# Attention in units of two heads inside a one-core hybrid layer (SSD, forgetting attention, PEER) on Trainium2

## The chip, the cores and the metric

The kernel runs on one core of one Trainium2 chip. The metric is the device time of one execution in microseconds (us). The engines are TensorE (PE; its weight loads are listed apart as PEld), VectorE (DVE), ScalarE (ACT), GpSimd (POOL) and SyncE (SP, used here to issue DMAs). Matmuls write to PSUM, which ACT and DVE read.

## The reference

For 512 tokens of width 2048 the layer computes, in float32:

```
h   = RMSNorm(x);  p = h @ w_in          (z | x,B,C | dt | q | k | v | forget logits)
y_A = Mamba-2 SSD of 16 heads
y_B = attention of 16 heads of 64:  for each block i of 128 queries
        s = q_i k[:qe]^T / 8 + C[t] - C[s],  C = cumsum(log sigmoid(f))
        p = softmax(s where t >= s);   out_i = p v[:qe]
x1  = x + concat(y_A, y_B) @ w_out
out = RMSNorm(x1 + PEER(RMSNorm(x1)))    (PEER: top-16 of 128*128 experts, 8 heads)
```

The change concerns y_B alone: 16 heads times 4 query blocks, block t (0 to 3) against its first 128(t+1) keys.

## The kernel before, in words

The large projections are computed to float32 accuracy with three matmuls: a weight piece is loaded by SP (`wload`, L73), split on ACT into a high part (L81) and on DVE into a low part (L82), and multiplied as high*high, low*high, high*low. `project_t` (L98) gives 128 output columns transposed, 16 steps of 3 matmuls of 128x512 (L103 to L105); `project_n` (L110) gives a 512-wide block of columns for all four token tiles (L117 to L119).

The attention (`fox`, L441) is a Python generator that is stepped from inside the projections, so that its PE work stands between projection matmuls. `front` (L229) computes the transposed q and k of two heads (a head pair, `hp`, 0 to 7) with `fox_qk` (L433). While it computes those of head pair hp+1, it calls `slot` after every fourth step (12 matmuls), 8 times in all, and each call advances `fox` by one step for head pair hp. The last head pair is stepped from `mid_first` (L499), the first block of the output projection, at each of its 16 steps (12 matmuls each), which also transposes the SSD output (`to_T`, L138) at its first four steps and splits the last attention rows (`split(15,7)`) when the attention is done.

One step of `fox` before starts one *unit*, (head, query block t), and advances those in flight:

- at its own slot: the score matmul (L453; 64 rows of the array, since the head has 64 elements, by 128(t+1) columns, float32, which the trace lists as two records) and the causal mask added by a bf16 matmul (L454) into the PSUM tile `at` (two buffers); then softmax: L456 and L459 on DVE, the exponential on ACT (L461), L462 and L463 on DVE;
- two slots later: t+1 transposes of the probabilities (L468, PSUM tile `tp`, two buffers) and their copy by ACT (L470);
- three slots later: t+1 value matmuls (L474, 64 columns of the array, two records each), summed in a second `tp` tile, and the copy to `mixf` by DVE (L476).

The two heads of a pair are done one after the other: four units of one, then four of the other. `crow`, the row of C of a head, is broadcast to all partitions by a DMA on SP (L487; two buffers, one per head). The order of the instructions on an engine is that of the program except where the scheduler of the language moved some, mostly around the last head pair. A matmul's form in the trace, as 64\*128, is the part of the array it uses (rows\*columns).

Of the kernel before, what the change touches and what calls it, by code (L numbers as in the profile page):

```python
# [9 lines left out]
F32 = mybir.dt.float32  # L10
# [3 lines left out]
AF = mybir.ActivationFunctionType  # L14
OP = mybir.AluOpType
AX = mybir.AxisListType
# [3 lines left out]
P = 128  # L20
T = 512
NT = 4
# [4 lines left out]
HD = 64  # L27
# [28 lines left out]
def bcast(ap, offset, dims):  # L56
    return bass.AP(tensor=ap.tensor, offset=ap.offset + offset, ap=[[0, P]] + dims)


class K:  # L60
# [380 lines left out]
    def fox(self, fp):  # L441


        nc = self.nc
        waiting = []

        def unit(hp, q, k, hh, t, crow):
            h = 2 * hp + hh
            rs = slice(hh * HD, (hh + 1) * HD)
            qe = (t + 1) * P  # L450
            ts_ = slice(t * P, qe)
            S = self.pp.tile([P, T], F32, name="at", tag="at", bufs=2)
            nc.tensor.matmul(S[:, :qe], q[rs, ts_], k[rs, :qe], start=True, stop=False, skip_group_check=True)  # L453
            nc.tensor.matmul(S[:, ts_], self.identb, self.maskb, start=False, stop=True, skip_group_check=True)  # L454
            pr = fp.tile([P, T], F32, name="pr", tag="pr", bufs=4)
            nc.vector.scalar_tensor_tensor(pr[:, :qe], S[:, :qe], self.nab[:, t, 32 + h:33 + h],  # L456
                                           crow[:, :qe], op0=OP.add, op1=OP.subtract)
            mx = fp.tile([P, 1], F32, name="mx", tag="mx", bufs=4)
            nc.vector.tensor_reduce(mx, pr[:, :qe], axis=AX.X, op=OP.max, negate=True)  # L459
            sm = fp.tile([P, 1], F32, name="sm", tag="sm", bufs=4)  # L460
            nc.scalar.activation(pr[:, :qe], pr[:, :qe], AF.Exp, bias=mx, accum_out=sm)  # L461
            nc.vector.reciprocal(sm, sm)  # L462
            nc.vector.tensor_scalar(pr[:, :qe], pr[:, :qe], sm, None, op0=OP.mult)  # L463
            yield
            yield
            tp = self.pp.tile([P, NT, P], F32, name="tp", tag="tp", bufs=2)
            for c in range(t + 1):
                nc.tensor.transpose(tp[:, c, :], pr[:, c * P:(c + 1) * P], self.ident)  # L468
            pT = fp.tile([P, NT, P], F32, name="pT", tag="pT", bufs=3)
            nc.scalar.activation(pT[:, :t + 1, :], tp[:, :t + 1, :], AF.Copy)  # L470
            yield
            yT = self.pp.tile([P, P], F32, name="tp", tag="tp", bufs=2)
            for c in range(t + 1):
                nc.tensor.matmul(yT[rs, :], self.vn[:, c, h * HD:(h + 1) * HD], pT[:, c, :],  # L474
                                 start=(c == 0), stop=(c == t), skip_group_check=True)
            nc.vector.tensor_copy(self.mixf[rs, hp, ts_], yT[rs, :])  # L476

        def advance():
            for u in waiting[:]:
                if next(u, 0) == 0:  # L480
                    waiting.remove(u)

        while True:
            hp, q, k = self.fox_in
            for hh in range(2):
                crow = fp.tile([P, T], F32, name="crow", tag="crow", bufs=2)
                nc.sync.dma_start(crow, bcast(self.rows, (32 + 2 * hp + hh) * T, [[1, T]]))  # L487
                for t in range(NT):
                    advance()
                    waiting.append(unit(hp, q, k, hh, t, crow))  # L490
                    next(waiting[-1])
                    yield
            if hp == 7:
                break
        while waiting:
            advance()
            yield

    def mid_first(self, es):  # L499


        nc, io = self.nc, self.io
        self.mixT = Th, Tl = self.new_T()

        def split(slot, c):
            nc.scalar.activation(Th[:, slot, :], self.mixf[:, c, :], AF.Copy)
            nc.vector.tensor_sub(Tl[:, slot, :], self.mixf[:, c, :], Th[:, slot, :].bitcast(F32))

        for c in range(6):
            split(c, c)  # L510

        def slot(kc):
            if kc < 4:
                for t in (2 * (kc % 2), 2 * (kc % 2) + 1):
                    self.to_T(self.mixn[:, t, (kc // 2) * 512:(kc // 2 + 1) * 512], t, Th, Tl, 7 + 4 * (kc // 2), 4)
            if kc == 4:
                split(6, 6)
            if next(self.fox_steps, 0) == 0 and not done:
                done.append(1)
                split(15, 7)  # L520

        done = []
        self.hp = self.pool(es, "h2p", side="right")
        self.xin = self.hp.tile([P, NT, 512], F32, name="xin", tag="h2n", bufs=1)
        for t in range(NT):
            nc.sync.dma_start(self.xin[:, t, :], io["x"][t][:, 0:512])
        return self.project_n(io["wo"][0], Th, Tl, slot)
# [31 lines left out]
    def mid_norm(self):  # L559

        nc, mp, x1 = self.nc, self.mp, self.x1
        self.T2 = [self.t2.tile([P, KC, DN], F32R, name=f"T2{n}", tag=f"T2{n}", bufs=1) for n in "hl"]
        self.T3 = [self.sx.tile([P, KC, P], F32R, name=f"T3{n}", tag="S", bufs=4) for n in "hl"]
        sm = mp.tile([P, NT], F32, name="sm2")
# [19 lines left out]
    def scores(self, tk):  # L584

        nc, io = self.nc, self.io
        kT = self.sx.tile([P, 16, P], F32, name="kT", tag="S", bufs=4)
        nc.sync.dma_start(kT, io["kT"])
# [3 lines left out]
        for c4 in range(4):  # L592
# [21 lines left out]
            def post(c4=c4, q=q, qn=qn):  # L614
# [3 lines left out]
                for j in range(4):  # L618
# [3 lines left out]
                    for t in range(NT):  # L622
                        nc.tensor.matmul(sp[:, t, :], q[j][:, t * P:(t + 1) * P], kT[:, hh, :], start=True, stop=True)
                    S = tk.tile([P, NT, P], F32, name="S", tag="tk_oh", bufs=3)
                    nc.scalar.activation(S, sp, AF.Copy)
# [462 lines left out]
```

## Time and profile before

| | |
|---|---|
| runs | median 3315.44 us of 3 (3312.17, 3315.44, 3324.38) |
| the profiled execution | 3313.59 us; span from first to last instruction 3311.9 us |
| PE | busy 3171.9 us, 96% |
| PEld | 2926.7 us, 88% |
| DVE | 2372.4 us, 72% |
| ACT | 1175.1 us, 35% |
| POOL | 882.6 us, 27% |
| mean granted TensorE clock | 0.988 of 2.4 GHz |

Busy time is an average over stages. The attention units lie between 436.4 us (the first score matmul) and 757.2 us (the end of the last value matmuls), a tenth of the span; what they are worth is read there. PE matmuls are pipelined and their listed durations overlap, so the cost of one is read from the distance between the starts of neighbours.

### The profile page before, as it was taken

The numbers are of one execution on the slowest core, as the hardware profiler recorded it, in microseconds if no ns is written. First come the engines' busy times: TensorE is split into PE (matmuls) and PEld (weight loads), VectorE is DVE, ScalarE is ACT, GpSimd is POOL, SyncE is SP. The second block draws the span as 40 slices with busy tenths as digits, with TensorE's granted clock in tenths as the row PEclk, the third lists the DMA queues.
The fourth block names the chain that finished last, engine by engine and source line by source line (L and its number), as shares of the span: only waits on it lengthen the run. The fifth ranks groups of instructions, "written<-read, shape, count | busy, mean of one in ns | idle before, by whom it ended". The sixth has DMA issues, their size and how long they took to land.

```text
span 3311.9 us, 45983 instructions
## 1 busy us (share of the span) xinstructions
PE 3171.9 (96%) x18153; PEld 2926.7 (88%) x18153; DVE 2372.4 (72%) x3315; ACT 1175.1 (35%) x1908; POOL 882.6 (27%) x535
## 2 busy tenths in 40 slices
PE   6999999999989988999998899999999999999998
PEld 4777776667789988999998899999999999999997
DVE  6474345553234699879877688898888998888885
ACT  3342233342232332364565432333332322323332
POOL 2000000001012054314111244434434454344430
PEclk9999999999989999999999999999999999999999
DMA  4333322215232255978877899999999999989992
GB/s 137 97 105 89 115 80 71 64 61 165 89 125 89 90 199 208 348 270 314 318 290 275 324 377 363 337 363 350 345 345 366 365 346 348 356 334 356 341 337 89
DMA packets 211400, 798.29 MB, mean 241 GB/s; under 512 B 19728, under 2 KB 27920, under 8 KB 166224
## 3 DMA queue, kind: packets, MB, share of 16 engines
q1 hardware_dynamic: 146352, 375.21, 32.9%
q0 software_dynamic: 55440, 375.15, 29.7%
q10 hardware_dynamic: 9392, 45.00, 3.3%
q8 instruction: 142, 2.33, 0.3%
q14 instruction: 74, 0.61, 0.1%
HBM read 748.98 MB, written 46.27 MB: 240 GB/s over the span
## 4 chain that ended last, share of the span: by engine, by line
PE 35%; DMA 7%; issue 5%; DVE 3%; POOL 2%; ACT 1%; DVEq 0%; POOLq 0%; ACTq 0%
PE mm L826 4%; PE mm L824 4%; PE mm L825 4%; PE mm L939 3%; PE mm L941 3%; PE mm L940 3%; DMA Gd<-gb 2%; PE at L941 2%; PE tp L941 1%; PE tp L939 1%; PE tp L940 1%; PE at L939 1%; PE at L940 1%; DMA A<-Ad 1%; DVE w_lo L82 1%
## 5 line engine op out<-in xcount | busy, mean ns | idle before, releaser
L81 ACT ACTIVATE w_hi<-w_raw 128x1024 fp32r<-128x1024 f32 x666 | 705.0, 1061 | 1552.2 <-PE mm L940 455.4
L82 DVE TENSOR_TENSOR w_lo<-w_raw,w_hi 128x1024 fp32r<-128x1024 f32 x648 | 815.6, 1270 | 533.6 <-ACT w_hi L81 523.8
L826 PE MATMUL mm<-T2h,w_lo 128*128 128x352 f32 x1664 | 543.8, 327 | 33.4 <-DVE w_lo L82 33.3
L824 PE MATMUL mm<-T2h,w_hi 128*128 128x352 f32 x1664 | 549.0, 330 | 0.8 <-ACT w_hi L81 0.8
L825 PE MATMUL mm<-T2l,w_hi 128*128 128x352 f32 x1664 | 540.7, 325 | 0.0
L753 POOL DMA_INDIRECT row<-in_u_dram,idx x128 | 207.4, 1620 | 555.8 <-DVE row L758 529.2
L826 PEld LDWEIGHTS mm<-T2h,w_lo 128*128 128x128 f32 x1664 | 316.4, 190 | 40.5 <-DVE w_lo L82 40.4
L770 DVE SCALAR_TENSOR_TENSOR x2g<-row,act,x2g 128x2048 f32<-128x2048 f32 x128 | 336.4, 2628 | 15.6 <-DMA row<-in_v_dram,idx 9.5
L939 PE MATMUL mm<-Wh,w_hi 128*128 128x352 f32 x1024 | 331.4, 324 | 0.0
L941 PE MATMUL mm<-Wh,w_lo 128*128 128x352 f32 x1024 | 331.1, 323 | 0.0
L940 PE MATMUL mm<-Wl,w_hi 128*128 128x352 f32 x1024 | 329.8, 322 | 0.0
L758 DVE SCALAR_TENSOR_TENSOR row<-row,h2n 128x2048 f32<-128x2048 f32 x128 | 305.5, 2401 | 19.0 <-DMA row<-in_u_dram,idx 19.0
L824 PEld LDWEIGHTS mm<-T2h,w_hi 128*128 128x128 f32 x1664 | 317.2, 191 | 1.1 <-ACT w_hi L81 1.1
L825 PEld LDWEIGHTS mm<-T2l,w_hi 128*128 128x128 f32 x1664 | 316.8, 190 | 0.0
L753 POOL DMA_INDIRECT row<-in_v_dram,idx x128 | 218.0, 1704 | 337.0 <-DVE x2g L770 309.9
L117 PE MATMUL mm<-w_hi,T_hi 128*128 128x512 f32 x512 | 205.0, 400 | 0.0
L119 PE MATMUL mm<-w_hi,T_lo 128*128 128x512 f32 x512 | 203.2, 397 | 0.0
L118 PE MATMUL mm<-w_lo,T_hi 128*128 128x512 f32 x512 | 201.9, 394 | 0.0
L940 PEld LDWEIGHTS mm<-Wl,w_hi 128*128 128x128 f32 x1024 | 194.0, 189 | 0.0
L941 PEld LDWEIGHTS mm<-Wh,w_lo 128*128 128x128 f32 x1024 | 193.5, 189 | 0.0
L939 PEld LDWEIGHTS mm<-Wh,w_hi 128*128 128x128 f32 x1024 | 192.9, 188 | 0.0
L103 PE MATMUL mm<-T_hi,w_hi 128*128 128x512 f32 x464 | 190.3, 411 | 0.0
(302 smaller groups left out, 6274.6 us busy)
## 6 DMA issues: line engine op xcount, KB each, us to landing
w_raw<-in_uT_dram SPq DMA_DIRECT2D x256, 512.0 KB
w_raw<-in_v_dram SPq DMA_DIRECT2D x256, 512.0 KB
w_raw<-in_wT_dram SPq DMA_DIRECT2D x58, 512.0 KB
Gd<-gb ACTq DMA_DIRECT2D x22, 1024.0 KB
G<-Gd POOLq DMA_DIRECT2D x32, 704.0 KB
w_raw<-in_wN_dram SPq DMA_DIRECT2D x32, 512.0 KB
w_raw<-in_wo_dram SPq DMA_DIRECT2D x32, 512.0 KB
w_raw<-in_wq_dram SPq DMA_DIRECT2D x32, 512.0 KB
```

The costliest lines, as they stand in the source:

```text
L81: nc.scalar.activation(hi, raw, AF.Copy)
L82: sub = eng.tensor_sub(lo, raw, hi.bitcast(F32))
L117: nc.tensor.matmul(ps[t], Th[:, kc, s], wh, start=(kc == 0), stop=False)
L753: nc.gpsimd.indirect_dma_start(out=row, out_offset=None, in_=src, in_offset=bass.IndirectOffsetOnAxis(ap=idx[:, j:j + 1], axis=0))
L758: nc.vector.scalar_tensor_tensor(row, row, 1.0, h, op0=OP.mult, op1=OP.mult, accum_out=act[:, j:j + 1])
L770: nc.vector.scalar_tensor_tensor(acc, row, act[:, j:j + 1], acc, op0=OP.mult, op1=OP.add)
L824: nc.tensor.matmul(ps, wh, Th[:, kc, :TD], start=(kc == 0), stop=False)
L825: nc.tensor.matmul(ps, wh, Tl[:, kc, :TD], start=False, stop=False)
L826: nc.tensor.matmul(ps, wl, Th[:, kc, :TD], start=False, stop=(kc == KC - 1))
L939: nc.tensor.matmul(ps[j], vh, wh, start=f, stop=False)
L940: nc.tensor.matmul(ps[j], vh, wl, start=False, stop=False)
L941: nc.tensor.matmul(ps[j], vl, wh, start=False, stop=l)
```

## The change

A unit is now (head pair, query block): both heads at once. At its slot it issues the two score matmuls one behind the other (head 0 on rows 0 to 63 of the array, head 1 on rows 64 to 127, each into an `at` tile of its own), then both masks and both softmaxes. Three slots later (before: two) come the transposes of both heads, four slots later the value matmuls, in which the heads alternate at each of the t+1 key blocks, head 0 on columns 0 to 63 and head 1 on columns 64 to 127 of one `tp` tile; one copy of 128 partitions to `mixf` replaces two of 64. A unit is started at every second slot, so that 4 units take the 8 slots that 8 units took. `crow` has three buffers in place of two, and both rows of a pair are fetched together. In `mid_first` the generator is stepped twice per step from the ninth on.

```diff
--- before.py
+++ after.py
@@ -441,39 +441,52 @@
     def fox(self, fp):
 
 
+
         nc = self.nc
         waiting = []
 
-        def unit(hp, q, k, hh, t, crow):
-            h = 2 * hp + hh
-            rs = slice(hh * HD, (hh + 1) * HD)
+        def unit(hp, q, k, t, crow):
             qe = (t + 1) * P
             ts_ = slice(t * P, qe)
-            S = self.pp.tile([P, T], F32, name="at", tag="at", bufs=2)
-            nc.tensor.matmul(S[:, :qe], q[rs, ts_], k[rs, :qe], start=True, stop=False, skip_group_check=True)
-            nc.tensor.matmul(S[:, ts_], self.identb, self.maskb, start=False, stop=True, skip_group_check=True)
-            pr = fp.tile([P, T], F32, name="pr", tag="pr", bufs=4)
-            nc.vector.scalar_tensor_tensor(pr[:, :qe], S[:, :qe], self.nab[:, t, 32 + h:33 + h],
-                                           crow[:, :qe], op0=OP.add, op1=OP.subtract)
-            mx = fp.tile([P, 1], F32, name="mx", tag="mx", bufs=4)
-            nc.vector.tensor_reduce(mx, pr[:, :qe], axis=AX.X, op=OP.max, negate=True)
-            sm = fp.tile([P, 1], F32, name="sm", tag="sm", bufs=4)
-            nc.scalar.activation(pr[:, :qe], pr[:, :qe], AF.Exp, bias=mx, accum_out=sm)
-            nc.vector.reciprocal(sm, sm)
-            nc.vector.tensor_scalar(pr[:, :qe], pr[:, :qe], sm, None, op0=OP.mult)
+            rs = [slice(hh * HD, (hh + 1) * HD) for hh in range(2)]
+            S = [self.pp.tile([P, T], F32, name="at", tag="at", bufs=2) for _ in range(2)]
+            for hh in range(2):
+                nc.tensor.matmul(S[hh][:, :qe], q[rs[hh], ts_], k[rs[hh], :qe], start=True, stop=False,
+                                 skip_group_check=True)
+            prs = []
+            for hh in range(2):
+                h = 2 * hp + hh
+                nc.tensor.matmul(S[hh][:, ts_], self.identb, self.maskb, start=False, stop=True,
+                                 skip_group_check=True)
+                pr = fp.tile([P, T], F32, name="pr", tag="pr", bufs=4)
+                nc.vector.scalar_tensor_tensor(pr[:, :qe], S[hh][:, :qe], self.nab[:, t, 32 + h:33 + h],
+                                               crow[hh][:, :qe], op0=OP.add, op1=OP.subtract)
+                mx = fp.tile([P, 1], F32, name="mx", tag="mx", bufs=4)
+                nc.vector.tensor_reduce(mx, pr[:, :qe], axis=AX.X, op=OP.max, negate=True)
+                sm = fp.tile([P, 1], F32, name="sm", tag="sm", bufs=4)
+                nc.scalar.activation(pr[:, :qe], pr[:, :qe], AF.Exp, bias=mx, accum_out=sm)
+                prs.append((pr, sm))
+            for pr, sm in prs:
+                nc.vector.reciprocal(sm, sm)
+                nc.vector.tensor_scalar(pr[:, :qe], pr[:, :qe], sm, None, op0=OP.mult)
             yield
             yield
-            tp = self.pp.tile([P, NT, P], F32, name="tp", tag="tp", bufs=2)
-            for c in range(t + 1):
-                nc.tensor.transpose(tp[:, c, :], pr[:, c * P:(c + 1) * P], self.ident)
-            pT = fp.tile([P, NT, P], F32, name="pT", tag="pT", bufs=3)
-            nc.scalar.activation(pT[:, :t + 1, :], tp[:, :t + 1, :], AF.Copy)
+            yield
+            pT = []
+            for pr, sm in prs:
+                tp = self.pp.tile([P, NT, P], F32, name="tp", tag="tp", bufs=2)
+                for c in range(t + 1):
+                    nc.tensor.transpose(tp[:, c, :], pr[:, c * P:(c + 1) * P], self.ident)
+                pT.append(fp.tile([P, NT, P], F32, name="pT", tag="pT", bufs=3))
+                nc.scalar.activation(pT[-1][:, :t + 1, :], tp[:, :t + 1, :], AF.Copy)
             yield
             yT = self.pp.tile([P, P], F32, name="tp", tag="tp", bufs=2)
             for c in range(t + 1):
-                nc.tensor.matmul(yT[rs, :], self.vn[:, c, h * HD:(h + 1) * HD], pT[:, c, :],
-                                 start=(c == 0), stop=(c == t), skip_group_check=True)
-            nc.vector.tensor_copy(self.mixf[rs, hp, ts_], yT[rs, :])
+                for hh in range(2):
+                    h = 2 * hp + hh
+                    nc.tensor.matmul(yT[rs[hh], :], self.vn[:, c, h * HD:(h + 1) * HD], pT[hh][:, c, :],
+                                     start=(c == 0), stop=(c == t), skip_group_check=True)
+            nc.vector.tensor_copy(self.mixf[:, hp, ts_], yT)
 
         def advance():
             for u in waiting[:]:
@@ -482,14 +495,17 @@
 
         while True:
             hp, q, k = self.fox_in
+            crow = []
             for hh in range(2):
-                crow = fp.tile([P, T], F32, name="crow", tag="crow", bufs=2)
-                nc.sync.dma_start(crow, bcast(self.rows, (32 + 2 * hp + hh) * T, [[1, T]]))
-                for t in range(NT):
-                    advance()
-                    waiting.append(unit(hp, q, k, hh, t, crow))
-                    next(waiting[-1])
-                    yield
+                crow.append(fp.tile([P, T], F32, name="crow", tag="crow", bufs=3))
+                nc.sync.dma_start(crow[hh], bcast(self.rows, (32 + 2 * hp + hh) * T, [[1, T]]))
+            for t in range(NT):
+                advance()
+                waiting.append(unit(hp, q, k, t, crow))
+                next(waiting[-1])
+                yield
+                advance()
+                yield
             if hp == 7:
                 break
         while waiting:
@@ -515,9 +531,10 @@
                     self.to_T(self.mixn[:, t, (kc // 2) * 512:(kc // 2 + 1) * 512], t, Th, Tl, 7 + 4 * (kc // 2), 4)
             if kc == 4:
                 split(6, 6)
-            if next(self.fox_steps, 0) == 0 and not done:
-                done.append(1)
-                split(15, 7)
+            for _ in range(1 if kc < 8 else 2):
+                if next(self.fox_steps, 0) == 0 and not done:
+                    done.append(1)
+                    split(15, 7)
 
         done = []
         self.hp = self.pool(es, "h2p", side="right")
```

How the instructions stand on PE in the regular part of the stage. Before, head pair 0 at the fourth slot: the value matmul of t=0, the transposes of t=1 and the score matmul of t=3 of one head, between two projection matmuls (L105 and L103); `mm` is the projection's PSUM tile, `vn` the values, `pr` the probabilities, `pT` their transpose.

```order
L105 MATMUL mm_2811<-T_hi_109,w_lo_2869 128x512
L474 MATMUL tp_2911<-pT_2886,vn_2183 64x128
L468 MATMUL tp_2914<-ident_69,pr_2858 128x128 x2
L453 MATMUL at_2919<-fk_2684,fq_2683 128x512
L454 LDWEIGHTS identb_74
L454 MATMUL at_2919<-maskb_76,identb_74 128x128
L103 MATMUL mm_2931<-T_hi_109,w_hi_2934 128x512
```

After, the slot that starts the unit t=3 of the same head pair: the four value matmuls of t=1, both score matmuls, both masks.

```order
L105 MATMUL mm_2929<-T_hi_109,w_lo_2999 128x512
L487 MATMUL tp_3014<-pT_2989,vn_2183 64x128
L487 MATMUL tp_3014<-pT_2994,vn_2183 64x128
L487 MATMUL tp_3014<-pT_2989,vn_2183 64x128
L487 MATMUL tp_3014<-pT_2994,vn_2183 64x128
L454 MATMUL at_3020<-fk_2684,fq_2683 128x512
L454 MATMUL at_3021<-fk_2684,fq_2683 128x512
L459 LDWEIGHTS identb_74
L459 MATMUL at_3020<-maskb_76,identb_74 128x128
L459 LDWEIGHTS identb_74
L459 MATMUL at_3021<-maskb_76,identb_74 128x128
L103 MATMUL mm_2929<-T_hi_109,w_hi_2998 128x512
```

And the slot behind it, where only transposes stand between the projection matmuls:

```order
L105 MATMUL mm_2929<-T_hi_109,w_lo_2999 128x512
L479 MATMUL tp_3054<-ident_69,pr_2957 128x128 x3
L479 MATMUL tp_3060<-ident_69,pr_2964 128x128 x3
L103 MATMUL mm_3069<-T_hi_109,w_hi_3072 128x512
```

What was met at every slot (values, transposes, scores, mask) is now met at every second one, without the transposes, which have the other slots to themselves.

At the last head pair the scheduler orders otherwise. Before, one of its slots (values t=1, transposes t=2, score t=0 of the second head):

```order
L474 MATMUL tp_5117<-pT_5082,vn_2183 64x128 x2
L468 MATMUL tp_5121<-ident_69,pr_5042 128x128 x3
L453 MATMUL at_5127<-fk_4570,fq_4569 128x128
L454 LDWEIGHTS identb_74
L454 MATMUL at_5127<-maskb_76,identb_74 128x128
```

After, one of its slots:

```order
L119 MATMUL mm_4832<-w_hi_5039,T_lo_4808 128x512
L479 MATMUL tp_5033<-ident_69,pr_4889 128x128
L487 MATMUL tp_5057<-pT_5031,vn_2183 64x128
L454 MATMUL at_5061<-fk_4518,fq_4517 128x384
L487 MATMUL tp_5057<-pT_5035,vn_2183 64x128
L454 MATMUL at_5062<-fk_4518,fq_4517 128x384
L459 LDWEIGHTS identb_74
L459 MATMUL at_5061<-maskb_76,identb_74 128x128
L459 LDWEIGHTS identb_74
L459 MATMUL at_5062<-maskb_76,identb_74 128x128
L117 MATMUL mm_4829<-w_hi_5039,T_hi_4807 128x512
```

There the two heads' matmuls do not stand side by side: value and score matmuls alternate, and two of the last pair's units (this one, t=2, and t=1) have their two score matmuls apart. All other units have the order shown above.

On SP, the order of the DMAs around the `crow` loads, before:

```order
L487 DMA crow_3100<-rows_444 128x512
L78 DMA w_raw_3380<-in_wT_dram 128x1024
L78 DMA w_raw_3456<-in_wT_dram 128x1024
L487 DMA crow_3248<-rows_444 128x512
L78 DMA w_raw_3528<-in_wT_dram 128x1024
```

and after:

```order
L501 DMA crow_3090<-rows_444 128x512
L501 DMA crow_3378<-rows_444 128x512
L78 DMA w_raw_3438<-in_wT_dram 128x1024
L78 DMA w_raw_3510<-in_wT_dram 128x1024
L78 DMA w_raw_3576<-in_wT_dram 128x1024
L78 DMA w_raw_3650<-in_wT_dram 128x1024
```

One `crow` load per two weight pieces became two loads per four pieces; the first of the two belongs to the second head of one pair, the other to the first head of the next. Behind the attention stage the order on all engines is the same as before.

## Rows read from the trace of the kernel before

**Rows 1.** The page, part 1: busy time, share of the span, instructions.
```profile
PE 3171.9 (96%) x18153; PEld 2926.7 (88%) x18153; DVE 2372.4 (72%) x3315; ACT 1175.1 (35%) x1908; POOL 882.6 (27%) x535
```

**Rows 2.** Busy time of each engine by stretch: window, length, engines, PEclk, DMA share, GB/s.
```profile
550.00:590.00 40.00, 40.00 (x188) 26.95 (x186) 20.31 (x47) 14.06 (x31) 0.00 (x0) 1.00 0.24 74
750.00:790.00 40.00, 40.00 (x179) 31.77 (x179) 12.56 (x14) 11.37 (x17) 5.06 (x4) 1.00 0.63 211
```

**Rows 3.** Timeline of PE inside the attention stage: start, us, engine, line, operation, tiles, count.
```profile
564.35 0.43 PE L474 MATMUL tp<-pT,vn 128*64 128x128 f32 x2
564.71 0.44 PE L468 MATMUL tp<-ident,pr 128*128 128x128 f32 x2
565.08 1.12 PE L453 MATMUL at<-fk,fq 64*128 64x512 f32 x2
566.13 0.23 PE L454 MATMUL at<-maskb,identb 128*128 128x128 bf16 x1
...
568.82 0.40 PE L105 MATMUL mm<-T_hi,w_lo 128*128 128x512 f32 x1
569.15 0.65 PE L474 MATMUL tp<-pT,vn 128*64 128x128 f32 x4
569.73 0.55 PE L468 MATMUL tp<-ident,pr 128*128 128x128 f32 x3
570.21 0.49 PE L453 MATMUL at<-fk,fq 64*128 64x128 f32 x2
570.62 0.23 PE L454 MATMUL at<-maskb,identb 128*128 128x128 bf16 x1
570.66 0.47 PE L103 MATMUL mm<-T_hi,w_hi 128*128 128x512 f32 x1
570.98 0.40 PE L104 MATMUL mm<-T_lo,w_hi 128*128 128x512 f32 x1
571.21 0.40 PE L105 MATMUL mm<-T_hi,w_lo 128*128 128x512 f32 x1
```

**Rows 4.** Timeline of all engines, the weight loads of one score matmul.
```profile
565.08 0.29 PEld L453 LDWEIGHTS at<-fk,fq 64*128 64x128 f32 x2 [0.17 <-issue]
```

**Rows 5.** Timeline of PE at the last head pair, transposes alone between projection matmuls.
```profile
721.63 0.40 PE L118 MATMUL mm<-w_lo,T_hi 128*128 128x512 f32 x1
721.87 0.39 PE L119 MATMUL mm<-w_hi,T_lo 128*128 128x512 f32 x1
722.10 0.27 PE L468 MATMUL tp<-ident,pr 128*128 128x128 f32 x1
722.12 0.48 PE L117 MATMUL mm<-w_hi,T_hi 128*128 128x512 f32 x1
722.44 0.40 PE L118 MATMUL mm<-w_lo,T_hi 128*128 128x512 f32 x1
```

**Rows 6.** Groups by line and shape, 436 to 760 us: busy us, mean ns, idle before.
```profile
L474 PE MATMUL tp<-pT,vn 128*64 128x128 f32 x320 | 48.7, 283 | 0.0
...
L82 DVE TENSOR_TENSOR w_lo<-w_raw,w_hi 128x1024 fp32r<-128x1024 f32 x33 | 40.3, 1221 | 3.8 <-ACT w_hi L81 3.6
...
L474 PEld LDWEIGHTS tp<-pT,vn 128*64 128x64 f32 x320 | 33.2, 136 | 23.3 <-issue 17.1 <-ACT pr L461 5.1 <-DVE T_lo L147 0.7
...
L453 PEld LDWEIGHTS at<-fk,fq 64*128 64x128 f32 x128 | 18.9, 185 | 10.8 <-issue 8.6 <-PE mm L104 0.4 <-ACT T_hi L506 0.2
...
L456 DVE SCALAR_TENSOR_TENSOR pr<-at,nab,crow 128x512 f32<-128x512 f32 x16 | 12.0, 747 | 0.3
L461 ACT ACTIVATE pr<-pr,mx 128x512 f32<-128x512 f32 x16 | 11.6, 725 | 27.6 <-DVE mx L459 27.6
...
L459 DVE TENSOR_REDUCE mx<-pr 128x1 f32<-128x512 f32 x16 | 11.0, 686 | 0.5
...
L470 ACT ACTIVATE pT<-tp 128x512 f32<-128x512 f32 x16 | 9.6, 597 | 12.1 <-PE tp L468 12.1
```

**Rows 7.** Timeline of SyncE's DMA queue in the attention stage.
```profile
567.23 0.33 SPq L487 DMA_DIRECT2D crow<-rows  x1
```

## The prediction

> **What bounds the kernel now.** I read the page's busy times first: PE is busy 96% of the span [rows 1]. An average over stages is not enough, so I cut the attention stage (436.4 to 757.2 us) out with the view of busy time by stretch. A stretch inside it has PE busy 40.00 of 40.00 us, DVE 20.31, ACT 14.06, the DMA engines 24%, and a granted clock of 1.00, the 2.4 GHz level; the stretch that follows is full on PE too, with DMA at 63% [rows 2]. So the stage is bound by PE, and every PE microsecond saved shortens it, as long as no new wait is made. A "busy" PE is not a PE that streams all the time, so I then read the starts of neighbouring matmuls in the timeline [rows 3]. A projection matmul of 512 columns starts 0.23 us after the one before it (570.98 to 571.21), the pace of streaming. Around the attention work the distances are larger, and they fall apart into a part that grows with the work and a fixed part:
>
> - values: 2 records take 0.36 us to the next start, 4 take 0.58: 0.11 per record and 0.145 fixed;
> - transposes: 2 take 0.37, 3 take 0.48: 0.11 each and 0.15 fixed;
> - score: 128 columns take 0.41, 512 take 1.05: 0.213 per 128 columns (two records of 0.107) and 0.20 fixed;
> - way in: the last L105 to the first value matmul 0.33 in place of 0.23: 0.09 fixed;
> - way out: mask to L103 0.04, then L103 to L104 0.32 in place of 0.23: 0.13 for the mask and the return.
>
> The fixed parts sum to 0.09 + 0.145 + 0.15 + 0.20 + 0.13 = 0.715 us a slot. They sit where the form changes (128\*128, 128\*64, 128\*128, 64\*128, 128\*128: four changes a slot): about 0.09 is there at every change, and the rest is a first weight load that nothing hides. For the score that load is 0.107: the two loads together take 0.29 and one takes 0.185, so the second starts 0.105 after the first, as soon as the first matmul streams [rows 4, 6]. The opposite case is in the trace as well: a transpose alone between projection matmuls, same form on both sides, leaves L118 to L118 (721.63 to 722.44) 0.81 us apart where three matmuls take 0.70: 0.11 for it, and no fixed part [rows 5].
>
> **The change, part by part.** *Fewer changes of form.* Before, 64 slots hold all four kinds. After, a pair of slots has one slot with values, scores and masks, and one with transposes alone. The first pays 0.09 + 0.145 + 0.20 + 0.13 and a second mask, which I take at 0.06, a quarter of a 512-column matmul (bounds: 0.04, mask to next start, and 0.23, its listed duration [rows 3]): 0.625. The second pays nothing fixed, by [rows 5]. Before, two slots paid 1.43. Saved: 0.805 us, times 32 units, 25.8 us. At the last head pair two units stand in pieces (the last two PE excerpts), with about 8 changes more than the rule, at some 0.16 each: 1.3 us back. **24.5 us** remain (about 253 changes become 103). The number of matmuls, transposes and their columns is unchanged.
>
> *Side by side.* The trace of before has no two neighbouring matmuls on different parts of the array, so what this gives must be bounded. Lower end: nothing, both stream one after the other. Upper end: everything runs two abreast; a head pair's scores stream 4.27 us (four records of 0.107, 0.213, 0.320, 0.427 for its four t), its values 40 records of 0.109, 4.36 us, and half of both, times 8, is 34.5 us. Between them lies what the order allows: a matmul is two records [rows 3, 6], and PE takes records in order, so A1 A2 B1 B2 can overlap only A2 with B1. A score pair then takes three record times instead of four, and saves one: 1.067 us a head pair, 8.5 us in all, less 0.5 for the two units that stand apart, less 0.9 for t=0, where four loads of 0.107 leave no room: **7.1 us**. Values go on alternating, A1 A2 B1 B2 A1 ..., so that 4m records take 2m+1 times (m key blocks): 1+3+5+7 = 16 record times a head pair, times 8 times 0.109, less one: **13.8 us**. I take these, because the forms are already half arrays and the loads of a following record are hidden behind the record before it (value records follow at 0.11 though a load takes 0.136 [rows 3, 6]).
>
> *Waits.* A pair's softmax at t=3 costs DVE 2(0.747+0.686) plus two scalings, taken as no longer than the first step's 0.747, and one weight split of 1.22 [rows 6]: 5.6 us in two slots, which last 9.6 us before (564.35 to 569.15 twice [rows 3]) and some 8.3 after (less 43/32). So the `at` tiles are free again and the probabilities stand ready within three slots. The copies to `mixf` fall from 64 to 32, on DVE, which is not the bound: nothing gained. Behind the late `crow` load on SP stand weight pieces. Before, it was issued once the last unit of the head before had been read, at 567.23, and used two heads later; now the second row of a pair is issued when the first head's last unit has been read, and used about two slots later, some 7 us for 256 KB at a 24% DMA share [rows 2, 7]. If it came late, DVE would read S late, seven times in all. In the SP order the weight pieces behind it belong to the pair after the next, so they stay early: nothing. What I do charge is `tp`: at the last head pair the transposes of two heads and of the SSD output meet in two buffers, and PE waits there about twice for two copies of up to 0.6 us [rows 6]: 2.2 us lost. After 757 us all engines keep their order, and PE is full: the gain carries to the end one for one; the bound on the other side, all of it lost to DMA at 63% [rows 2], has no wait of PE to speak for it.
>
> *Sum*, against the profiled execution's own 3313.6 us, 1.9 below the median of 3315.4: 24.5 + 7.1 + 13.8 - 2.2 = 43.2 saved, **3270 us**.
>
> **The rivals.** *No overlap at all.* PE may stream one matmul at a time whatever part of the array it uses. For it: nothing in this trace shows two abreast. Against it: nothing either. 3313.6 - 24.5 + 2.2 = 3291 us. Chance 0.24.
>
> *One kind only.* Rows alone: 3284; columns alone: 3277.5. A variant: loads on other columns of the same rows are not hidden. Then each of the 127 changes of head among the value matmuls shows a load of 0.05 (0.145 less the change of 0.09), 6.4 us, and with rows overlapping the time is 3290. Chance of all these 0.17. The Trainium skill ("TensorE: Matmul & The Clock Gate", Part 3, "The mechanism") says that weight loads overlap running matmuls only when the row group differs, which speaks against the values here, whose heads share all rows; within one tile the trace disagrees, with value records following at 0.11 us.
>
> *Each change of head is a change of form* (the change doesn't do what it says). PE might drain and reload at every switch of rows or columns: 127 times 0.145 and 30 times 0.20 = 24.4 us, 3316 us, no change. Chance 0.07.
>
> *Slower.* The same place, dearer: each of these 157 switches drains (0.094) and then shows the whole listed load, 0.136 for values and 0.185 for scores [rows 6]: 127 x 0.23 + 30 x 0.28 = 37.6 us, 3329 us. It decides from 22.3/157 = 0.14 us a switch upwards. Against it: no load in the trace shows in full, the score's shows 0.107 of its 0.185. Chance 0.02.
>
> **How the numbers follow.** Both kinds overlapping has 0.50, so 3270 is the forecast. The range has to take in the cases without overlap (3291, and 3 us of further waits) above, and below a part of the way to full two abreast (3313.6 - 24.5 - 34.5 + 2.2 = 3257): 3261 to 3294. It leaves out the cases of 0.09 and the tails. About 0.5%, 16.6 us, is what a measurement of this kernel can tell from no change. All cases but the last two lie below 3299: faster 0.90, same 0.08, slower 0.02.
>
> **What would show it.** The stage from first score to last value matmul should shrink from 321 to about 278 us (299 without overlap), with PE still full. In a start-of-unit slot at m=2, eight value records should take some 0.145 + 5 x 0.11 = 0.70 us to the first score matmul (1.02 serial); the pair of 512-column scores some 1.5 us to the mask (1.9 serial), with the third record starting together with the second. A slot of transposes should cost 0.11 each. The forecast is wrong if the value records of two heads still start 0.11 apart, if a wait on `at`, `tp` or `crow` of over 0.3 us stands in the regular slots, or if the stage shrinks and a later one grows.

## The result and the profile after

The changed kernel took 3260.8 us (median of 6 runs, 3255.1 to 3266.0) against 3319.5 us for the kernel before (6 runs, 3312.2 to 3324.4): a ratio of 0.9825, 95% interval 0.9807 to 0.9843. The forecast was 3270, with a range of 3261 to 3294; the median lies on its lower edge (0.2 us under it, with runs on both sides). The profiled execution of the changed kernel took 3255.1 us.

All of the gain must be found in the attention stage or it is not the one that was forecast. To compare stages that hold the same projection work, the stage is counted here from the first score matmul through the 816 projection matmuls that start behind it, to the start of the next one (the last value matmul lies inside in both kernels). The view of busy time by stretch, for the kernel before over just this stretch (window, length, then PE, PEld, DVE, ACT, POOL busy, PEclk, DMA share, GB/s):

```profile
436.40:762.93 326.53, 326.53 (x1521) 222.12 (x1521) 168.71 (x370) 120.15 (x256) 0.00 (x0) 1.00 0.23 71
```

and for the changed kernel, the same stretch and the window that stands in [rows 2]:

```profile
438.50:708.60 270.10, 269.65 (x1522) 200.25 (x1521) 151.49 (x338) 109.20 (x256) 0.00 (x0) 1.00 0.27 85
550.00:590.00 40.00, 40.00 (x228) 29.50 (x227) 22.77 (x51) 15.33 (x38) 0.00 (x0) 1.00 0.29 86
```

The stage shrank from 326.53 to 270.10 us, by 56.4, and PE is still full in it at the same granted clock. PE's busy time over the span fell with it (3171.9 in [rows 1]):

```profile
PE 3115.0 (96%) x18153; PEld 2905.4 (89%) x18153; DVE 2355.3 (72%) x3283; ACT 1163.4 (36%) x1908; POOL 893.3 (27%) x535
```

Between the profiled executions (3313.6 and 3255.1) lie 58.5 us. The 2.1 us that the stage does not hold are made of two pieces: the stretch before the first score took 2.1 more (436.4 to 438.5 us), and the work behind the stage took 4.2 less (2549.0 to 2544.8). Neither can be put down to the change: in the eleven profiles of the changed kernel and its variants below, the first score starts between 435.3 and 443.2 us and the work behind the stage takes from 2544.8 to 2555.6 us, while the stage of the changed kernel is 270.1 us in all three of its own profiles. Experiments are therefore judged by the stage, which repeats to a few hundredths of a microsecond.

The timeline of PE in the changed kernel, rows that answer to [rows 3] and [rows 5] (start, us, engine, line, operation, tiles, count):

```profile
459.08 0.66 PE L487 MATMUL tp<-pT,vn 128*64 128x128 f32 x8
459.67 1.13 PE L454 MATMUL at<-fk,fq 64*128 64x512 f32 x4
460.73 0.28 PE L459 MATMUL at<-maskb,identb 128*128 128x128 bf16 x2
...
467.28 0.88 PE L487 MATMUL tp<-pT,vn 128*64 128x128 f32 x12
468.08 0.49 PE L454 MATMUL at<-fk,fq 64*128 64x128 f32 x4
468.51 0.29 PE L459 MATMUL at<-maskb,identb 128*128 128x128 bf16 x2
...
475.26 1.09 PE L487 MATMUL tp<-pT,vn 128*64 128x128 f32 x16
476.28 0.70 PE L454 MATMUL at<-fk,fq 64*128 64x256 f32 x4
...
479.67 0.39 PE L105 MATMUL mm<-T_hi,w_lo 128*128 128x512 f32 x1
479.90 0.38 PE L479 MATMUL tp<-ident,pr 128*128 128x128 f32 x2
480.03 0.48 PE L103 MATMUL mm<-T_hi,w_hi 128*128 128x512 f32 x1
480.35 0.40 PE L104 MATMUL mm<-T_lo,w_hi 128*128 128x512 f32 x1
```

Eight value records of two heads take 0.59 us to the first score (459.08 to 459.67); four of one head took 0.58 before. The pair of 512-column scores takes 1.06 to the mask, one such score took 1.05. The pair of 128 columns takes 0.43, one took 0.41. Twelve value records take 0.80, sixteen 1.02. A second head costs next to nothing: both kinds run fully two abreast. Two transposes alone in their slot leave L105 to L104 0.68 apart (479.67 to 480.35) where two projection matmuls take 0.47: 0.11 each, nothing fixed, as forecast.

How the records stand can be seen by cutting the timeline 0.04 us behind the start of a row of value matmuls. In the kernel before, only one record has started by then:

```profile
573.65 0.32 PE L474 MATMUL tp<-pT,vn 128*64 128x128 f32 x1
```

In the changed kernel two have:

```profile
475.26 0.33 PE L487 MATMUL tp<-pT,vn 128*64 128x128 f32 x2
```

These two cannot be the two records of one matmul, which start 0.16 apart (two records of L474 end 0.43 behind the first start [rows 3], and the second lasts 0.27). They belong to the two heads. The weight loads behave alike: the four loads of a score pair take 0.30 us, the two of a single score 0.29 [rows 4]:

```profile
476.28 0.30 PEld L454 LDWEIGHTS at<-fk,fq 64*128 64x128 f32 x4 [0.17 <-issue]
```

### The profile page after: what moved, and what is told of

Same layout as the page of the kernel before. It is cut to its first block, busy times and chain, and to the rows that moved or that the text cites. A ratio compares the mean times of both kernels' runs of the same rounds, so it can differ in the third digit from the quotient of the medians.

```text
span 3253.4 us, 45911 instructions
## 1 busy us (share of the span) xinstructions
PE 3115.0 (96%) x18153; PEld 2905.4 (89%) x18153; DVE 2355.3 (72%) x3283; ACT 1163.4 (36%) x1908; POOL 893.3 (27%) x535
## 4 chain that ended last, share of the span: by engine, by line
PE 71%; DVE 10%; DMA 9%; issue 7%; POOL 2%; ACT 1%; DVEq 0%; POOLq 0%; ACTq 0%; SPq 0%
PE mm L843 5%; PE mm L841 5%; PE mm L842 5%; PE mm L117 3%; PE mm L119 3%; PE mm L118 3%; PE mm L956 3%; PE mm L958 3%; PE mm L957 3%; PE mm L103 3%; PE mm L105 3%; PE mm L104 3%; DVE w_lo L82 3%; DMA Gd<-gb 2%; PE at L958 2%
## 5 line engine op out<-in xcount | busy, mean ns | idle before, releaser
L103 PE MATMUL mm<-T_hi,w_hi 128*128 128x512 f32 x464 | 190.5, 411 | 0.0
```

## The experiments

Stage as above; time is the median of the runs, the ratio is to the kernel before on the same chip.

| run | stage us | against 270.1 | time us (runs) | ratio (95%) |
|---|---|---|---|---|
| before | 326.5 | +56.4 | 3319.5 (6) | |
| changed | 270.1 | 0 | 3260.8 (6) | 0.9825 (0.9807 to 0.9843) |
| e1 heads in sequence | 276.3 | +6.2 | 3268.1 (4) | 0.9844 (0.9825 to 0.9863) |
| e2 same rows | 286.1 | +16.0 | 3277.5 (4) | 0.9872 (0.9849 to 0.9896) |
| e3 same columns | 286.6 | +16.5 | 3272.5 (4) | 0.9856 (0.9834 to 0.9878) |
| e4 neither | 302.9 | +32.8 | 3293.7 (4) | 0.9916 (0.9900 to 0.9933) |
| e5 values with the transposes | 273.8 | +3.7 | 3267.4 (4) | 0.9844 (0.9817 to 0.9871) |
| e6 blocks of two | 270.6 | +0.5 | 3262.2 (1) | |
| e7 merged units | 265.6 | -4.5 | 3261.0 (5) | 0.9819 (0.9797 to 0.9842) |
| e8 changed, beside e7 | 270.1 | 0 | 3263.7 (5) | 0.9822 (0.9799 to 0.9845) |
| e9 merged units, second | 265.6 | -4.5 | 3258.0 (5) | 0.9816 (0.9797 to 0.9834) |
| e10 changed, beside e9 | 270.1 | 0 | 3264.5 (5) | 0.9840 (0.9820 to 0.9859) |

### What is the rows', what is the columns', what is neither's (e2, e3, e4)

e2 takes the different rows away:

```diff
-                nc.tensor.matmul(S[hh][:, :qe], q[rs[hh], ts_], k[rs[hh], :qe], start=True, stop=False,
+                nc.tensor.matmul(S[hh][:, :qe], q[rs[0], ts_], k[rs[0], :qe], start=True, stop=False,
```

> The changed kernel with both score matmuls of a unit reading q and k of head 0, so both on rows 0 to 63 (the attention of head 1 then has head 0's scores). Nothing else differs. Theory: the scores run two abreast because they are on different rows; on the same rows each pair takes twice its streaming time: 1.067 x 2 us a head pair, 8 pairs, less the two units whose scores stand apart anyway: plus 16.0 us, stage 286.1 against 270.1. Rival: the score pair is no shorter because of the rows (its gain is the saved form change alone): 270.1.

Measured: 286.08, plus 15.99. The pair of 512 columns now takes 1.92 us to the mask in place of 1.06:

```profile
459.95 1.98 PE L454 MATMUL at<-fk,fq 64*128 64x512 f32 x4
461.87 0.28 PE L459 MATMUL at<-maskb,identb 128*128 128x128 bf16 x2
```

e3 takes the different columns away:

```diff
-                    nc.tensor.matmul(yT[rs[hh], :], self.vn[:, c, h * HD:(h + 1) * HD], pT[hh][:, c, :],
-                                     start=(c == 0), stop=(c == t), skip_group_check=True)
-            nc.vector.tensor_copy(self.mixf[:, hp, ts_], yT)
+                    nc.tensor.matmul(yT[rs[0], :], self.vn[:, c, h * HD:(h + 1) * HD], pT[hh][:, c, :],
+                                     start=(c == hh == 0), stop=(c == t and hh == 1), skip_group_check=True)
+            for hh in range(2):
+                nc.vector.tensor_copy(self.mixf[rs[hh], hp, ts_], yT[rs[0], :])
```

> The changed kernel with the value matmuls of both heads on columns 0 to 63, added up in one place and copied to both heads' rows (both heads then have the sum); the heads still alternate. Theory: values run two abreast because they are on different columns; here 2m matmul times instead of m: 10 x 0.218 x 8 = 17.4 us more, less 0.2 for the unit that stands in pieces, stage 287.3. Rival: alternation in the queue is what helps, the columns do not matter: 270.1.

Measured: 286.55, plus 16.46. Sixteen value records take 1.89 us to the first score; the alternation of the heads alone gives nothing (0.145 and sixteen times 0.109 make 1.89):

```profile
473.59 1.96 PE L487 MATMUL tp<-pT,vn 128*64 128x128 f32 x16
475.48 0.70 PE L454 MATMUL at<-fk,fq 64*128 64x256 f32 x4
```

e3 also adds both heads' sums up in one place, so by itself it leaves open whether the shared place or the shared columns make the records queue. The merged units of e9 below answer that: there the sums of t=0 and t=1 stand in different places of one tile, and the six records of each half still follow one another, in 0.81 us where six records of one sum take 0.80:

```profile
487.50 0.88 PE L492 MATMUL tp<-pT,vn 128*64 128x128 f32 x12
488.31 1.13 PE L455 MATMUL at<-fk,fq 64*128 64x512 f32 x4
```

The 0.8 us by which e3 stays under the expected 287.3 belong to the last head pair, where the scheduler put its instructions in another order than in the changed kernel: 102 changes of form stand in the stage in place of 104, in e4 too.

e4 is both edits together.

> Both of the last two at once: no two matmuls on different parts of the array, but the units of two heads, the order and the changes of form of the changed kernel. Theory: what is left against the kernel before is the fewer changes of form alone, 24.5 us less some 1.5 of waits: stage 303.3 (270.1 + 16.0 + 17.2), time some 23 us below the kernel before. Rival: the two overlaps hide the same time, or something else than the changes of form makes the rest: the stage of before, 326.5, or less than 295.

Measured: 302.93. In the view by stretch:

```profile
435.67:738.60 302.93, 302.45 (x1521) 226.99 (x1521) 160.54 (x370) 109.58 (x256) 0.00 (x0) 1.00 0.24 77
```

So the gain of 56.4 us falls into three parts that add up: 23.6 from the kernel before to e4, which has the units of two heads and nothing side by side; 16.0 for the rows; 16.5 for the columns (together 56.1; e4 less the changed kernel is 32.8, the two alone 32.45; the 0.3 that are left over lie at the last head pair, with its other order). The time agrees: e4 is 0.84% below the kernel before, with an interval that excludes no change.

### Must the two heads alternate? (e1, e6)

e1 turns the loop round:

```diff
-            for c in range(t + 1):
-                for hh in range(2):
+            for hh in range(2):
+                for c in range(t + 1):
                     h = 2 * hp + hh
```

> The changed kernel with one loop turned round: all value matmuls of head 0 first, then all of head 1, still on columns 0 to 63 and 64 to 127. The stage is counted from the first score matmul to the 816th projection matmul behind it: 326.5 us before, 270.1 us in the changed kernel. Theory 1 (a matmul starts in program order, beside the one before it if that is on another half of the array; a later one never overtakes a waiting one): only the last of head 0 and the first of head 1 overlap, a unit with m key blocks takes 2m-1 matmul times of 0.218 instead of m; plus 6 x 0.218 x 8 = 10.5 us, stage 280.6. Theory 2 (each half takes its own matmuls as soon as they are in PE's queue, ahead of waiting ones): no change, 270.1. Theory 3 (nothing overlaps unless the heads alternate record by record): plus 10 x 0.218 x 8 = 17.4 us, 287.5.

Measured: 276.28, plus 6.2: none of the three. The rows of one head pair show why (t=1, 2 and 3, each with the next kind of matmul behind it):

```profile
455.88 0.66 PE L487 MATMUL tp<-pT,vn 128*64 128x128 f32 x8
456.47 1.13 PE L454 MATMUL at<-fk,fq 64*128 64x512 f32 x4
...
464.08 1.15 PE L487 MATMUL tp<-pT,vn 128*64 128x128 f32 x12
465.16 0.49 PE L454 MATMUL at<-fk,fq 64*128 64x128 f32 x4
...
472.34 1.58 PE L487 MATMUL tp<-pT,vn 128*64 128x128 f32 x16
473.86 0.70 PE L454 MATMUL at<-fk,fq 64*128 64x256 f32 x4
```

Eight records (two key blocks) take 0.59 us, as when they alternate, although all four of head 0 stand before those of head 1. Twelve take 1.08 (0.80 alternating, 1.45 on the same columns in e3's trace), sixteen 1.52 (1.02 and 1.89). The saving against the same columns stops at about 0.37 us, some three and a half record times. The same timeline, cut 0.29 us behind the first start of the twelve and 0.51 behind that of the sixteen, counts four and six records:

```profile
464.08 0.60 PE L487 MATMUL tp<-pT,vn 128*64 128x128 f32 x4
```

```profile
472.34 0.82 PE L487 MATMUL tp<-pT,vn 128*64 128x128 f32 x6
```

One half alone would have started three and five by then (starts at 0, 0.16, 0.27, 0.38, 0.49). So head 1's first record starts with head 0's third of six, and with its fifth of eight; in the short unit it starts with the first of four. Each time three records of head 0 are still waiting before it. PE did start a record ahead of waiting ones, but of three at most. In matmuls of two records each the same rows read: one matmul of head 0 has started its first record, and one whole matmul waits; whether PE counts records or matmuls, these runs do not tell. That was a new theory, so e6 tests it with blocks of two key blocks:

```diff
-            for c in range(t + 1):
-                for hh in range(2):
+            for c0 in range(0, t + 1, 2):
+                for hh in range(2):
+                    for c in range(c0, min(c0 + 2, t + 1)):
...
```

> The changed kernel with the value matmuls in blocks: two key blocks of head 0, two of head 1, the next two of head 0, and so on. Theory (from the run in sequence: a record starts beside another half's work while at most three records of the other head stand waiting before it): four records of one head in a row, the first starts, three wait, so the other head's start at once; a unit with m=4 takes 1.03 us from its first value record to the next kind of matmul, as in the changed kernel; stage 270.1. Rival (a matmul never starts before one that stands ahead of it): m=4 takes five matmul times in place of four, 1.24 us, m=2 0.80 in place of 0.59; stage some 4 us longer.

Measured: 270.64, where the rival asked for some 4 us more. Eight records 0.59 us, sixteen 1.07:

```profile
457.42 0.66 PE L488 MATMUL tp<-pT,vn 128*64 128x128 f32 x8
458.01 1.13 PE L454 MATMUL at<-fk,fq 64*128 64x512 f32 x4
...
473.62 1.14 PE L488 MATMUL tp<-pT,vn 128*64 128x128 f32 x16
474.69 0.70 PE L454 MATMUL at<-fk,fq 64*128 64x256 f32 x4
```

The sixteen are 0.05 us over those of the changed kernel (1.02): in the second half of the row, by the starts of its records, one head runs half a record (0.057 us) behind the other. This fits a half that had to stop and shows one load of 64 columns again, but that was not tried.

### What a change of form costs (e5), and a version with fewer (e7, e9)

e5 moves the value matmuls one slot on:

```diff
             yield
+            yield
             yT = self.pp.tile([P, P], F32, name="tp", tag="tp", bufs=2)
```

> The changed kernel with the value matmuls one slot later, in the slots of the transposes: the same matmuls, the same overlaps, but 28 changes of form more (132 in place of 104 by the order). Theory: a change of form costs PE some 0.14 to 0.15 us wherever it stands (0.09 and a first load of 64 or 128 columns): plus 3.9 us, stage (first score matmul to the 816th projection matmul behind it) 274.0 against 270.1. Rival: what costs is the interruption of the projection, once per slot, however many forms are in it: each slot is interrupted as before, 270.1.

Measured: 273.80, plus 3.7, 0.13 us for each of 28 changes (104 become 132 in the traces too). By itself this does not exclude the rival: the scheduler split some of the transposes, and the projection is interrupted 86 times in e5's stage, 68 in the changed kernel's. But transposes alone leave no fixed cost (above), and the other kernels part the two causes: the kernel before has 74 interruptions and 254 changes, e4 has 70 and 102 and is 23.6 us shorter; e9 below has 70 and 78 and is 4.5 shorter than the changed kernel. It is the forms that cost, not the interruption.

```profile
436.06:709.86 273.80, 273.80 (x1521) 196.60 (x1521) 147.92 (x338) 112.78 (x256) 0.00 (x0) 1.00 0.26 83
```

This points to a version with fewer changes. e7 makes one unit of t=0 and t=1: their scores stand side by side in one `at` tile of each head (128 and 256 of its 512 columns), their transposes in one `tp` tile, their value sums in another. Three units per head pair start at slots 0, 3 and 6 of the eight:

```diff
-        def unit(hp, q, k, t, crow):
+        def unit(hp, q, k, ts, crow):
+            off = [0, P] if len(ts) == 2 else [0]
...
+            for o, t in zip(off, ts):
+                for hh in range(2):
+                    nc.tensor.matmul(S[hh][:, o:o + (t + 1) * P], q[rs[hh], t * P:(t + 1) * P],
+                                     k[rs[hh], :(t + 1) * P], start=True, stop=False, skip_group_check=True)
...
+        plan = {0: ((0, 1), 4, 6), 3: ((2,), 4, 5), 6: ((3,), 4, 5)}
```

The numbers of the plan are the unit's query blocks and the slots after which its transposes and its values follow (the last unit of the last head pair has 3 and 4).

> The units of t=0 and t=1 of a head pair as one (scores of both in the one score tile of a head, 384 columns; one slot of transposes; one of values), so three starts per head pair in place of four, spread over the same 8 slots: 78 changes of form in place of 104, the same matmuls. Theory (changes of form are what is left to save): stage about 264 us against 270.1, time some 6 us below the changed kernel. Rival: the longer bursts make PE wait for the softmax or for score and transpose tiles and give it back: 270 or more.

> The changed kernel once more, beside the merged units on the same chip: some 58 us below the kernel before, stage 270.1 us.

Measured: stage 265.58 beside 270.10 of the changed kernel, times 3261.0 and 3263.7, too near each other to tell apart. In e7 the attention of t=0 is left without its scores: the matmul of t=1 carries the flag that starts a new sum, and after it the mask of t=0, in other columns of the same tile, replaces the scores in place of being added to them. (The reference with the scores of t=0 put at zero lies a relative 0.0564 from the full one, and so does e7's output.) e9 gives the flag to t=0 alone:

```diff
-                                     k[rs[hh], :(t + 1) * P], start=True, stop=False, skip_group_check=True)
+                                     k[rs[hh], :(t + 1) * P], start=(o == 0), stop=False, skip_group_check=True)
```

> The merged units again, the score of t=1 issued without the flag that starts a new sum (that flag, given on other columns of the same score tile, is what this run suspects of having dropped the scores of t=0: with start=False on columns not yet written since the t=0 matmul, both should be kept). The same instructions otherwise, so the stage of the first merged run, 265.6 us, against 270.1 of the changed kernel; time 2 to 5 us below the changed kernel on the same chip. Rival: the stage grows back to 270 because the sums now depend on each other.

> The changed kernel beside it: stage 270.1 us, some 58 us below the kernel before.

Measured: e9's stage is the same 265.59 us, and 4.5 below the changed kernel beside it:

```profile
436.41:702.00 265.59, 264.82 (x1521) 199.03 (x1521) 145.01 (x330) 110.31 (x240) 0.00 (x0) 1.00 0.27 86
```

```profile
436.06:706.14 270.08, 269.63 (x1521) 200.07 (x1521) 151.49 (x338) 109.28 (x256) 0.00 (x0) 1.00 0.27 85
```

By the order, 26 changes of form are gone: 0.17 us each. The times are 3258.0 (3255.0 to 3259.1) and 3264.5 (3262.3 to 3270.8), five runs each whose ranges do not meet; against the kernel before the ratios are 0.9816 and 0.9840. By the stage e9 is 4.5 us, 0.14%, under the changed kernel. The times fit that, but e7, with the same stage, could not be told from e8 by them, so the gain of the whole kernel rests on these two sets of runs alone. The expected 264 was missed by 1.6 us. It asked for 0.23 us a change, more than any experiment found; at e4's price, 23.6 us for 152 changes, 26 are worth 4.0 us.

## Why the prediction was right, and where it was off

- **PE bounds the stage and what it saves there reaches the end.** Right: PE is full before and after, and the 56.4 us of the stage make the 58.5 us between the profiled executions, within the scatter of the rest.
- **Fewer changes of form, 24.5 us, less 2.2 of waits.** Right: e4, which has nothing else, saves 23.6. e5 prices 28 changes at 0.13 each, e9 26 at 0.17; the forecast's 24.5 us for 150 changes are 0.16 for one, read from the starts of neighbours. The traces have 254 changes before and 104 after, where the forecast had about 253 and 103. Transposes in a slot of their own cost 0.11 each and nothing more.
- **Side by side.** Both kinds overlap, as in the case with half of the chances; both rows and columns are needed for it (e2, e3). Its size was off. The step that failed is "PE takes records in order, so A1 A2 B1 B2 can overlap only A2 with B1". That was assumed, for no row of before shows it. In its place, the other half's first record starts with A1: the scores saved 16.0 us, not 7.1, and the values 16.5, not 13.8. The signs that the prediction named for its size, 0.70 us for the eight value records and 1.5 for the pair of 512-column scores, came out as 0.59 and 1.06. The upper end of the bound (34.5 for both) was nearly the truth: 32.5. The sum with these measured terms, 23.6 + 16.0 + 16.5 = 56.1 against the forecast 43.2, holds nearly all of what the prediction missed in the profiled execution.
- **The 0.9 us for t=0, "where four loads of 0.107 leave no room".** Wrong for the same reason: the loads of the two heads run two abreast too, 0.30 us for four, and the pair of 128 columns takes 0.43 us to the mask where one took 0.41.
- **Waits.** The forecast charged 2.2 us to `tp` at the last head pair. If the 24.5 for the forms are right, that was too much by about 1.3, since e4 saves 23.6 of them; no run parts the two terms. In the list of waits, those on a copy of `pT` sum to 1.9 us at most, since a matmul and its load may list the same time (1.0 us in the kernel before; the columns are: waiting, tile and line, released by, us in total, times, longest us):

```profile
PEld tp L144 <- ACT pT L481: 1.0, 2, 0.7
...
PE tp L144 <- ACT pT L481: 0.5, 1, 0.5
PEld tp L479 <- ACT pT L481: 0.4, 1, 0.4
```

  `at` and `crow` hold nothing up: in the same list no wait of PE on either stands.
- **The rivals.** No overlap (3291), each switch of head as dear as a change of form (3316) and dearer (3329) are excluded by the rows themselves, one kind alone by e2 and e3, which each cost some 16 us. The variant in which loads on other columns of the same rows are not hidden, which gave 3290, did not hold: the heads' values share all rows, and sixteen records take 1.02 us. The Trainium skill ("TensorE: Matmul & The Clock Gate", Part 3, "The mechanism") also says that matmuls start strictly in program order. Here the trace differs: in e1 a record starts before three that stand ahead of it.

The interval of the ratio allows a gain of 1.6 to 1.9%; the forecast 3270 is 1.4% under the median then at hand, 3315.4. That median rose to 3319.5 with more runs; a forecast of 43 us less would read 3276 against it, so the step that was mis-sized weighs more than the two times side by side tell. Of the saving, 43.2 us were forecast and 58.7 measured between the medians; that the measured time stands at the edge of the range and not some 4 us under it is luck, since the kernel before also read 4 us higher with more runs.

## What to carry to other kernels

Count the changes of form on PE before counting matmuls: here each costs 0.13 to 0.17 us, more than a record of 128 columns (0.11), and some 150 fewer of them were worth 24 us. Matmuls that fill half of the array's rows or columns came nearly free in pairs here, in float32 (no other type was tried), where the two stood on different halves and near each other in the program (alternating, or within three records). The scores of a pair went to different tiles and its values to different partitions of one tile; other arrangements were not tried. The price of such a pair in the trace is that of one: read it from the distance to the next kind of matmul, not from busy time.

## What was not expected of the hardware

- Two float32 matmuls on different halves ran record by record together, their starts within 0.04 us, with their weight loads, so that sixteen records take 1.02 us where the same sixteen on one half take 1.89.
- Program order was not strict on PE. With the heads in sequence, the second head's first record started early, with three records of the first (one whole matmul and the second half of another) still waiting; the gain then stopped at some 0.37 us a unit, for three key blocks as for four.
- The flag that starts a new sum in PSUM reaches beyond the columns of its own matmul: in e7 it dropped the scores of t=0 in the other columns of the tile, in e9, without it, they stay. The Trainium skill ("PSUM — Partial Sum Buffer", "The four PSUM rules") says that it clears the written marks of the whole bank in the partitions it writes, and that the next matmul without it overwrites there; e7 and e9 agree.
